# Three pairs of token tiles of the vs projection as seven block products, with weight sums built by adding transfers into SBUF

## The chip, the cores and the metric

The kernel runs on one core of one Trainium2 chip. The metric is the device time of that core in microseconds (us). Before the change the median of three runs is 911.1 us (910.71 to 911.81).

In what follows the engines carry the names of the profile: PE is the matrix engine, DVE the vector engine, ACT the scalar engine, POOL and SP the two engines that issue most of the DMA transfers.

## The reference, cut to what matters

```python
h = rmsnorm(x, norm_g[l])
proj = h @ w_in[l]
q, k, v, za, u, vs, zs, gm = jnp.split(proj, IN_SPLITS, axis=-1)
...
sgo = chunked_spatial_gating(jax.nn.gelu(u, approximate=False),
                             jax.nn.gelu(vs, approximate=False),
                             sg_w[l], sg_b[l], sg_ln_g[l], sg_ln_b[l])
```

`x` has 1024 tokens of 1024 features, in float32. The change concerns one part of `proj`: `vs`, 1024 columns, that is h (1024 x 1024) times a 1024 x 1024 block of `w_in`, followed by a gelu. The gating then layer-normalises vs over its features and mixes it over positions; u, the next projection, is computed right after vs.

## The kernel before

**Precision.** Each float32 operand is split into a high part and a low part. One ACT copy rounds the operand to the high part (`hi`), one DVE subtraction leaves the rest (`lo`); the helper `split` (lines 170 to 178) does both. A product then takes three matmuls: hi x hi, hi x lo and lo x hi. One matmul covers 128 tokens, a contraction of 128 and 512 output columns.

**Seven products.** Most projections of the kernel already use the scheme of Strassen and Winograd on 2 x 2 blocks (`gemm_pair`, line 405, `product`, line 382). The blocks of h are called b11, b21, b12, b22: feature half 0 or 1, token half 0 or 1. Five of the seven products need sums of those blocks or the last of them. The sums, t1 to t4, are made by `make_forms` (line 817) out of unrounded transposed copies of h (f11, f21, f12, f22); they serve the u projection, right after vs, and those that follow.

**vs, before.** vs is computed plainly, with 8 token tiles x 2 column halves x 8 contraction steps x 3 matmuls = 384 matmuls.

- *Column half 0* is computed while the eight tiles of x arrive. `normed_tile` (line 667) loads a tile of x, normalises and scales it (`scaled_part`, line 650, with the gain taken from the two PSUM banks `g_in`), transposes it on PE, casts it into hi and lo (`cast_part`, line 661) and copies the unrounded transpose to f11 to f22. `vs_gemm` (line 700) then runs the 24 matmuls of a tile into one PSUM bank, and line 706 copies it to `xh`. The weights of column half 0 lie split in SBUF in the slots T_t1 and T_t2 (`vs_split`).
- *Column half 1* follows in the loop at lines 857 to 869. There the eight tiles hold all eight PSUM banks at once; the outer loop runs over four weight tiles (`vs_weights`, line 795: one transfer of 512 KB, one cast, one subtraction), the inner one over the token tiles, with 6 matmuls for each. The work of `aside` (gelu of column half 0, `make_forms`) is emitted after every second tile.

**What orders the work.** The tile framework emits instructions by the order of the program unless they must wait, and puts later ones that are ready into gaps; each engine then executes its own queue strictly in order. Buffers of a tag are handed out in rotation: `wh` and `wl` (split weights) and `wr` (raw tiles of x and w) have three each, `s` two, `x` five; PSUM has four tags (mm, o, sc, tp) of two banks each. A transfer into a buffer waits for the last reader of its former content.

**Transfers.** Plain loads go through SP's queue (`copy_to`, line 227). Transfers that add to their destination go through POOL's queue (`add_to`, line 224). POOL's queue also carries the `early` steps (`early_job`, line 332, and line 516): sums of weight quarters for projections much later, made in DRAM. Each early step waits for the latest matmul of vs at the time it was emitted (`pace`), so that they are spread over PE's work; `part_of_early` (line 524) emits one of them at every second call.

**After vs** come the layer norm's statistics (`statistics_of`, line 901), `normalize` (line 905) and the mixing matmuls (`mix`, line 939), interleaved with `gemm_pair` of u, whose first weights are split in the last part of vs.

Of the kernel before, what the change touches and what calls it, by code (L numbers as in the profile page):

```python
# [32 lines left out]
P = 128  # L33
D = 1024
# [20 lines left out]
def hybrid_tile(  # L55
# [541 lines left out]
    for j in range(4):  # L597
# [25 lines left out]
    def quarter_of(t, j):  # L623

        if t >= 4 and j == 0:
            return b12[t - 4]
        return [v[:, :, tokens(t)] for v in hb[("b11", "b21", "b22")[j if t < 4 else 2]]]
# [22 lines left out]
    def scaled_part(t, j, xt, r):  # L650
        cs = half_of(j)
        scale = nc.vector.scalar_tensor_tensor(xt[:, cs], xt[:, cs], r[:], g_in[j][:], op0=ALU.mult, op1=ALU.mult)
        scalings.append(scale)
        pt = bank("o" if t == 1 else "tp")
        for i in range(4):
            k = j * 4 + i
            turn = nc.tensor.transpose(pt[:, i * P : (i + 1) * P], xt[:, k * P : (k + 1) * P], ident[:])
        p3 = pt[:].rearrange("p (k c) -> p k c", k=4)
        return p3, (f[f"f{j + 1}{t // 4 + 1}"][:, :, tokens(t)], p3), scale, turn
# [7 lines left out]
    def normed_tile(t, scale=None):  # L667
        xt, r = scale or scale_of(t)
        if t == 4:
            hb.update(new_b(("b22",)))  # L670
            f.update((n, slot(at, dt=F32)) for n, at in (("f12", "t4h"), ("f22", "t3h")))
        for j in range(2):
            p3, copy, _, _ = scaled_part(t, j, xt, r)
            cast_part(t, j, p3)
            nc.scalar.copy(*copy)

    def vs_step(acc, t, k, wh, wl):

        hi, lo = (v[:, k % 4, :] for v in quarter_of(t, k // 4))
        for n, (lt, rt) in enumerate(((hi, wh), (hi, wl), (lo, wh))):  # L680
            mm = nc.tensor.matmul(acc, lt, rt, start=k == 0 and n == 0, stop=k == KC - 1 and n == 2)  # L681
        return mm

    vs_w, vs_casts = [], []

    def split_vs(c):
# [11 lines left out]
        return cast, None  # L698

    def vs_gemm(t, middle=None):  # L700
# [19 lines left out]
    def first_tiles():  # L720
# [59 lines left out]
        high, low = cast_part(1, 1, p3)  # L780
        in_order(roots[2], high)
        vs_gemm(1, {4: lambda: both(3, "hl"), 5: lambda: normed_tile(2, third)})
        nc.scalar.copy(xh[:, 0, 0:HALF], acc0[:])
# [11 lines left out]
    def vs_weights(c):  # L795
        raw = raw_tile()
        nc.sync.dma_start(raw[:], w[W_VS + 4 + c])
        hi = mtile([P, D], F32R, "wh", 3)
        lo = mtile([P, D], F32R, "wl", 3)
        split(hi[:], lo[:], raw[:])  # L800
        return hi, lo

    def statistics(t, half):
        nc.vector.bn_stats(stats[:, t, half, :], xh[:, t, half_of(half)])

    def gelu_of(t):
        two = xh[:, t : t + 2, 0:HALF]
        after(nc.scalar.activation(two, two, AF.Gelu), roots[NT - 1])
        for i in range(2):
            statistics(t + i, 0)  # L810

# [5 lines left out]
    def make_forms():  # L817
# [17 lines left out]
        last = []  # L835
        for c in range(0, 4, 2):
            cs = slice(c, c + 2)
            v = mtile([P, 2, HALF], F32, "s", 2)
            nc.vector.tensor_sub(v[:], f11[:, cs, :], f21[:, cs, :])
            last.append(v)  # L840
            yield
        hb.update(new_b(("t3",)))
# [3 lines left out]
        hb.update(new_b(("t4",)))  # L846
        for c in range(0, 4, 2):
            form("t4", last[c // 2][:], c)
            yield

    accs = [bank(tag) for tag in ("mm", "mm", "o", "o", "sc", "sc", "tp", "tp")]
    aside = [lambda t=t: gelu_of(t) for t in range(0, NT, 2)]
    forms = make_forms()
    aside[1:1] = [lambda: next(forms, None)] * 2
    aside += [lambda: next(forms, None)] * 11
    weights = [vs_weights(0), vs_weights(1)]
    for c in range(4):
        if c + 2 < 4:
            weights.append(vs_weights(c + 2))
        for t in range(NT):  # L860
            wh, wl = weights[c]
            for k in range(2):
                ks = half_of(k)
                pace[0] = vs_step(accs[t][:], t, 2 * c + k, wh[:, ks], wl[:, ks])
            part_of_early()
            if c == 3:
                nc.scalar.activation(xh[:, t, HALF:D], accs[t][:], AF.Gelu)
            if aside and t % 2:
                aside.pop(0)()
    while aside:  # L870
# [1239 lines left out]
```

## Time and profile before

| | us |
|---|---|
| Median of three runs | 911.1 |
| The profiled execution, whole | 910.52 |
| Its span, first to last instruction | 908.7 |
| PE busy in the span | 898.6 |
| DVE busy | 693.3 |
| ACT busy | 528.6 |
| POOL busy | 145.6 |
| End of the vs projection on PE | 104.67 after the span's start |

All views of the profile come from one execution. Times are counted from the start of the span. A busy time is the time in which an instruction of that engine was executing; DMA-issuing instructions do not count. A view of "waits" names for each idle stretch of an engine what ended it; a "chain" is followed back from the last instruction through what released each step; a view of "windows" gives busy times for stretches of the span, with the number of instructions in brackets, the clock granted to PE, the mean busy share of the 16 DMA engines and the bytes that they moved.

### The profile page before, as it was taken

How to read it: one execution, taken by the hardware profiler on the slowest of the kernel's cores; microseconds unless marked ns; L12 is line 12 of the kernel's file. 1: busy time of each engine (PE TensorE's matmuls, PEld its weight loads, DVE VectorE, ACT ScalarE, POOL GpSimd, SP SyncE). 2: the span in 40 equal slices, each digit the busy share in tenths (PEclk: the TensorE clock that was granted, in tenths of full speed). 3: DMA queues.
4: the chain of work that ended last, by engine and by line, in shares of the span. 5: the costliest groups of instructions: out<-in, count | busy, mean ns of one | idle time of the engine just before them, and what ended most of it. 6: DMA issues, size and time to landing. Idle time of an engine off the chain costs nothing.

```text
span 908.7 us, 13248 instructions
## 1 busy us (share of the span) xinstructions
PE 898.6 (99%) x4305; PEld 748.9 (82%) x4305; DVE 693.3 (76%) x1238; ACT 528.6 (58%) x1060; POOL 145.6 (16%) x221
## 2 busy tenths in 40 slices
PE   8999999999999999999999999999999999999996
PEld 5788888888888888888888888888888888888885
DVE  6874776656678677888888887656698699579986
ACT  7942443334444557888778887434476485367443
POOL 2002222213011001222211110011100111210012
PEclk9999999999999999999999999999999999999999
DMA  6428788877778889999999994875568666998633
GB/s 232 139 93 216 170 163 190 178 186 222 241 263 267 268 265 319 266 256 270 270 344 252 269 241 144 300 261 182 171 208 301 221 203 179 283 323 282 201 116 116
DMA packets 129748, 206.10 MB, mean 227 GB/s; under 512 B 12716, under 2 KB 60848, under 8 KB 129680
## 3 DMA queue, kind: packets, MB, share of 16 engines
q1 hardware_dynamic: 108008, 146.27, 49.8%
q0 software_dynamic: 21376, 58.73, 26.7%
q8 instruction: 34, 0.56, 0.2%
q10 hardware_dynamic: 296, 0.27, 0.1%
q14 instruction: 34, 0.28, 0.1%
HBM read 148.46 MB, written 90.31 MB: 263 GB/s over the span
## 4 chain that ended last, share of the span: by engine, by line
PE 97%; DMA 1%; ACT 1%; DVE 0%; SPq 0%; issue 0%; ACTq 0%
PE ps_mm L395 44%; PE ps_o L395 27%; PE ps_mm L681 5%; PE ps_tp L395 4%; PE ps_sc L1291 3%; PE ps_sc L395 2%; PE ps_tp L943 2%; PE ps_tp L1372 2%; PE ps_o L1432 2%; PE ps_tp L681 1%; PE ps_sc L681 1%; PE ps_o L681 1%; PE ps_o L1440 1%; PE ps_tp L1382 1%; DMA T_t3h<-in_w_dram 1%; DMA wr<-in_x_dram 1%
## 5 line engine op out<-in xcount | busy, mean ns | idle before, releaser
L177 ACT CAST wh<-s 128x1024 fp32r<-128x1024 f32 (+1 forms) x78 | 78.1, 1003 | 82.6 <-PE ps_mm L395 29.0
L178 DVE TENSOR_TENSOR wl<-s,wh 128x1024 fp32r<-128x1024 f32 (+1 forms) x78 | 91.4, 1171 | 20.0 <-ACT wh L177 19.8
L178 DVE TENSOR_TENSOR wl<-wr,wh 128x1024 fp32r<-128x1024 f32 (+1 forms) x64 | 60.4, 945 | 59.1 <-ACT wh L177 58.9
L177 ACT CAST wh<-wr 128x1024 fp32r<-128x1024 f32 (+1 forms) x64 | 53.0, 830 | 77.5 <-PE ps_mm L395 34.5
L1332 ACT ACTIVATE pr<-ps_sc,sm 128x192 f32<-128x192 f32 (+2 forms) x128 | 51.3, 408 | 24.6 <-DVE sm L1323 21.6
L338 POOL DMA_DIRECT2D sums<-in_w_dram x48 | 36.7, 864 | 178.4 <-PE ps_mm L395 83.4
L395 PE MATMUL ps_o<-T_b22h,wh 128*128 128x512 f32 x148 | 59.0, 398 | 0.0
L395 PE MATMUL ps_o<-T_t1h,wh 128*128 128x512 f32 x148 | 58.0, 392 | 0.0
L395 PE MATMUL ps_o<-T_b22h,wl 128*128 128x512 f32 x148 | 57.8, 391 | 0.0
L395 PE MATMUL ps_o<-T_t1h,wl 128*128 128x512 f32 x148 | 57.8, 391 | 0.0
L395 PE MATMUL ps_o<-T_b22l,wh 128*128 128x512 f32 x148 | 57.8, 390 | 0.0
L395 PE MATMUL ps_o<-T_t1l,wh 128*128 128x512 f32 x148 | 57.7, 390 | 0.0
L395 PE MATMUL ps_mm<-T_t4h,wh 128*128 128x512 f32 (+1 forms) x144 | 55.9, 388 | 0.0
L395 PE MATMUL ps_mm<-T_t4l,wh 128*128 128x512 f32 (+1 forms) x144 | 55.4, 384 | 0.0
L395 PE MATMUL ps_mm<-T_t4h,wl 128*128 128x512 f32 (+1 forms) x144 | 55.3, 384 | 0.0
L395 PE MATMUL ps_mm<-T_t2h,wh 128*128 128x512 f32 x140 | 55.3, 395 | 0.0
L395 PE MATMUL ps_mm<-T_b11h,wh 128*128 128x512 f32 x140 | 55.1, 394 | 0.0
L395 PE MATMUL ps_mm<-T_t3h,wh 128*128 128x512 f32 x140 | 54.8, 391 | 0.0
L395 PE MATMUL ps_mm<-T_b11l,wh 128*128 128x512 f32 x140 | 54.7, 391 | 0.0
L395 PE MATMUL ps_mm<-T_b11h,wl 128*128 128x512 f32 x140 | 54.6, 390 | 0.0
L395 PE MATMUL ps_mm<-T_t3h,wl 128*128 128x512 f32 x140 | 54.6, 390 | 0.0
L395 PE MATMUL ps_mm<-T_t2h,wl 128*128 128x512 f32 x140 | 54.6, 390 | 0.0
(420 smaller groups left out, 2473.9 us busy)
## 6 DMA issues: line engine op xcount, KB each, us to landing
wr<-in_w_dram SPq DMA_DIRECT2D x80, 256.0 KB
sums<-in_w_dram POOLq DMA_DIRECT2D x24, 512.0 KB, 6.7
s<-sums SPq DMA_DIRECT2D x24, 512.0 KB
wr<-in_w_dram SPq DMA_DIRECT2D x16, 512.0 KB
q_hl<-qhl SPq DMA_DIRECT2D x16, 512.0 KB
q<-q_hl SPq DMA_DIRECT2D x64, 128.0 KB
y_dr<-x POOLq DMA_DIRECT2D x28, 256.0 KB, 6.4
sums<-in_w_dram POOLq DMA_DIRECT2D x24, 256.0 KB, 8.0
```

The source lines that it names most:

```text
L177: hi_casts.append(nc.scalar.copy(hi, src))
L178: return nc.vector.tensor_sub(lo, src, hi.bitcast(F32))
L338: return lambda: paced(nc.gpsimd.dma_start(dst, src, accum_op=op))
L395: mm = nc.tensor.matmul(acc, lt, rt, start=fresh and k == 0 and n == 0, stop=k == 3 and n == 2, skip_group_check=True,)
L681: mm = nc.tensor.matmul(acc, lt, rt, start=k == 0 and n == 0, stop=k == KC - 1 and n == 2)
L943: nc.tensor.matmul(pm[:, t * P : (t + 1) * P], xh[:, half * 4 + t, g * P : (g + 1) * P], bias[-1][1][:, g % 2, :], start=True, stop=True,)
L1291: nc.tensor.matmul(sc[:, i, lo:hi], q_of[:, c, i * P : (i + 1) * P], kt[:, f, lo:hi], start=f == 0, stop=f == 1,)
L1332: nc.scalar.activation(st.pr[:, i, place_of(c, lo, hi)], st.sc[c][:, i, lo:hi], AF.Exp, bias=st.nmax[:, c, i : i + 1], scale=-1.0, accum_o ...
L1372: nc.tensor.transpose(st.inner[0:wide, at : at + P], st.pr[:, i, place_of(c, 64 if st.t else P, 192)], ident[:])
L1382: nc.tensor.transpose(st.ends[0:wide, i * P : (i + 1) * P], st.pr[:, i, P : P + wide], ident[:])
L1432: nc.tensor.matmul(st.po[:], lt, rt, start=i == 0, stop=False, skip_group_check=True)
L1440: nc.tensor.matmul(st.po[:, cols(c)], ends[:, c, vs], st.b[:, cols(c)], start=False, stop=c == 1, skip_group_check=True)
```

## The change

- Token tiles p and p + 4 form a pair, for p = 1, 2, 3. The three pairs are computed with seven block products instead of eight. Tiles 0 and 4 stay plain.
- Column half 0 is now computed plainly for tiles 0 to 4 only. For tiles 1 to 3 the two contraction halves go to separate banks: the first half's product stays in its bank (`vs_acc`) for later use, a copy of it and the second half's product (bank `p1`, shared by the three) are added by DVE into `xh`.
- Column half 1 is computed plainly for tiles 0 and 4 only (`others`), with four weight tiles.
- Then come five products for each of the three pairs, in the order t1, t2, t3, b22, t4: the outer loop runs over the forms, then over two weight tiles for each, then over the three pairs, with 6 matmuls for each. `after_form` combines each finished product with `xh` on ACT or DVE and applies the gelu.
- The five products need five weights: W12+W22, W11+W12+W22, W11+W12, the sum of all four, and W22, in two tiles each. Three of them are built up in place in two SBUF tiles (`chain`, tag `s`): W12 is loaded, used by `others`, then W22, W11 and W21 are added one after another by adding transfers of 512 KB, each after the split of the former content. W11+W12 is built by a load and an adding transfer in a raw tile.
- The gain is copied from PSUM to SBUF (`g_sb`, two ACT copies) and taken from there from tile 2 on. The feature half 0 of tiles 5 to 7 is no longer cast to hi and lo. The t4 form is made in four x tiles instead of two s tiles. `make_forms` is emitted earlier.

```diff
-    b12 = [
-        [v[:].rearrange("p (a k c) -> p a k c", a=2, k=4)[:, i] for i in range(2)]
-        for v in (mtile([P, D], F32R, "s", 2) for _ in range(2))
-    ]
-    b12 = [(hi, mtile([P, 4, P], F32R, "x", 5)[:]) for two in b12 for hi in two]
+    b12 = [mtile([P, 4, P], F32R, "x", 5)[:] for _ in range(2)]
+    g_sb = htile([P, D], F32, "g_sb")
...
+            if t <= 4 or j:
+                cast_part(t, j, p3)
...
     def vs_gemm(t, middle=None):
-        acc = bank("mm")
+        acc = vs_acc[t] = bank("o" if t in (2, 3) else "mm")[:]
+        part = acc
+        if t == 1:
+            vs_acc["p1"] = bank("sc")[:]
+        dst = xh[:, t, 0:HALF]
         for k in range(KC):
             if middle and k in middle:
                 middle[k]()
-            vs_step(acc[:], t, k, *vs_w[k])
-        nc.scalar.copy(xh[:, t, 0:HALF], acc[:])
+            if t < 4 and k == 4:
+                nc.scalar.copy(dst, acc)
+                part = vs_acc["p1"]
+            vs_step(part, t, k, *vs_w[k], (0, KC - 1) if t == 4 else (k & 4, k | 3))
+        if t == 4:
+            nc.scalar.copy(dst, acc)
+        else:
+            nc.vector.tensor_add(dst, dst, part)
...
-    for t in range(NT):
+    chain = []
+    for t in range(5):
         if t > 1:
             vs_gemm(t)
         if t + 3 < NT:
             normed_tile(t + 3)
+        if t == 2:
+            for c in range(2):
+                chain.append(mtile([P, D], F32, "s", 2))
+                copy_to(chain[c][:], w[W_VS + 4 + c])
...
+    def of_chain(c, nxt=None):
+        two = vs_weights(chain[c][:])
+        if nxt is not None:
+            add_to(chain[c][:], w[W_VS + nxt])
+        return two
+
+    def of_raw(first, second=None):
+        raw = raw_tile()
+        copy_to(raw[:], w[W_VS + first])
+        if second is not None:
+            add_to(raw[:], w[W_VS + second])
+        return vs_weights(raw[:])
+
+    makers = [lambda c=c: of_chain(c, 6 + c) for c in range(2)]
+    makers += [lambda c=c: of_raw(6 + c) for c in range(2)]
+    makers += [lambda c=c: of_chain(c, c) for c in range(2)]
+    makers += [lambda c=c: of_chain(c, 2 + c) for c in range(2)]
+    makers += [lambda c=c: of_raw(c, 4 + c) for c in range(2)]
+    makers += [lambda c=c: of_chain(c) for c in range(2)]
+    makers += [lambda c=c: of_raw(6 + c) for c in range(2)]
...
+    for _ in range(2):
+        more_weights()
+    others = {t: bank("sc")[:] for t in (0, 4)}
     for c in range(4):
-        if c + 2 < 4:
-            weights.append(vs_weights(c + 2))
-        for t in range(NT):
-            wh, wl = weights[c]
+        more_weights()
+        wh, wl = weights[c]
+        for t in (0, 4):
             for k in range(2):
-                ks = half_of(k)
-                pace[0] = vs_step(accs[t][:], t, 2 * c + k, wh[:, ks], wl[:, ks])
-            part_of_early()
+                pace[0] = vs_step(others[t], t, 2 * c + k, wh[:, half_of(k)], wl[:, half_of(k)])
             if c == 3:
-                nc.scalar.activation(xh[:, t, HALF:D], accs[t][:], AF.Gelu)
-            if aside and t % 2:
-                aside.pop(0)()
+                nc.scalar.activation(xh[:, t, HALF:D], others[t], AF.Gelu)
+            part_done()
+
+    t5s = {1: bank("tp")[:], 2: bank("tp")[:], 3: vs_acc[4]}
+
+    def after_form(name, p, acc):
+        q1, q2 = xh[:, p + 4, 0:HALF], xh[:, p + 4, HALF:D]
+        if name == "t1":
+            nc.scalar.mul(q2, acc, -1.0)
+        elif name == "t2":
+            nc.scalar.copy(q1, acc)
+        elif name == "t3":
+            nc.vector.tensor_sub(q2, q2, acc)
+            gelu_of(p + 4, 1, 1)
+        elif name == "b22":
+            nc.vector.tensor_add(q1, q1, acc)
+            gelu_of(p + 4, 1)
+        else:
+            nc.scalar.activation(xh[:, p, HALF:D], acc, AF.Gelu, scale=-1.0)
+
+    for s, name in enumerate(("t1", "t2", "t3", "b22", "t4")):
+        into = t5s if name in ("t1", "b22") else vs_acc
+        for c in range(2):
+            more_weights()
+            wh, wl = weights[4 + 2 * s + c]
+            hi, lo = hb[name]
+            for p in (1, 2, 3):
+                for k in range(2):
+                    at = 2 * c + k
+                    pace[0] = step_of(
...
+                if c:
+                    after_form(name, p, into[p])
+                part_done()
```

`part_done` calls `part_of_early` and emits the next piece of `aside`; `more_weights` makes the next entry of `makers`, so that weights are requested two weight tiles ahead of their use. `step_of` holds the three matmuls of a step.

More of the change, by code (lines that the diff above doesn't have):

```diff
@@ L673, in normed_tile, with step_of, vs_step @@
             p3, copy, _, _ = scaled_part(t, j, xt, r)
-            cast_part(t, j, p3)
+            if t <= 4 or j:
+                cast_part(t, j, p3)
             nc.scalar.copy(*copy)
-    def vs_step(acc, t, k, wh, wl):
+    def step_of(acc, hi, lo, wh, wl, first, last):
+        for n, (lt, rt) in enumerate(((hi, wh), (hi, wl), (lo, wh))):
+            mm = nc.tensor.matmul(
+                acc, lt, rt, start=first and n == 0, stop=last and n == 2, skip_group_check=True
+            )
+        return mm
+    def vs_step(acc, t, k, wh, wl, ends=(0, KC - 1)):
         hi, lo = (v[:, k % 4, :] for v in quarter_of(t, k // 4))
-        for n, (lt, rt) in enumerate(((hi, wh), (hi, wl), (lo, wh))):
-            mm = nc.tensor.matmul(acc, lt, rt, start=k == 0 and n == 0, stop=k == KC - 1 and n == 2)
-        return mm
+        return step_of(acc, hi, lo, wh, wl, k == ends[0], k == ends[1])
     vs_w, vs_casts = [], []
@@ L781, in first_tiles @@
         in_order(roots[2], high)
+        for j in range(2):
+            nc.scalar.copy(g_sb[:, half_of(j)], g_in[j][:])
         vs_gemm(1, {4: lambda: both(3, "hl"), 5: lambda: normed_tile(2, third)})
@@ L846, in make_forms @@
         hb.update(new_b(("t4",)))
[L847 to L852, printed above, removed]
-    forms = make_forms()
-    aside[1:1] = [lambda: next(forms, None)] * 2
-    aside += [lambda: next(forms, None)] * 11
-    weights = [vs_weights(0), vs_weights(1)]
+        hi, lo = hb["t4"]
+        for c in range(4):
+            split(hi[:, c, :], lo[:, c, :], last[c][:])
+            if c % 2:
+                yield
```

60 lines of the change are left out of this document (43 added, 17 removed).

## The prediction

> **What bounds the kernel now.** I read the page first, then the waits of PE, then the chain that ended last, and then the busy times in windows around the vs projection.
>
> ```profile
> span 908.7 us, 13248 instructions
> PE 898.6 (99%) x4305; PEld 748.9 (82%) x4305; DVE 693.3 (76%) x1238; ACT 528.6 (58%) x1060; POOL 145.6 (16%) x221
> PE 97%; DMA 1%; ACT 1%; DVE 0%; SPq 0%; issue 0%; ACTq 0%
> ...
> PE ps_o L591 <- DVE T_b22l L106: 1.5, 1, 1.5
> PE ps_mm L754 <- ACT T_t2h L692: 0.7, 1, 0.7
> PE ps_sc L599 <- DVE wh L585: 0.6, 1, 0.6
> PE ps_tp L657 <- ACT T_t3h L675: 0.2, 1, 0.2
> PE ps_mm L754 <- ACT T_b11h L663: 0.2, 1, 0.2
> ```
>
> PE is busy 99% of the span and makes 97% of the chain. The second part of the fence is the view of waits for PE alone: in the whole execution PE waits five times, 3.2 us in all, each time on lines of the first tiles. So a matmul that is left out saves its own duration, as long as nothing else is late. The chain and the windows show the place:
>
> ```profile
> 44.81 19.06 PE ps_mm L681 x84
> ...
> 101.95 2.72 PE ps_tp L681 x12
> 104.67 2.72 PE ps_mm L395 x12
> ...
> 121.24 1.78 PE ps_tp L943 x16
> ```
>
> ```profile
> 0.00:44.80 44.80, 41.53 (x202) 30.68 (x203) 34.59 (x77) 38.66 (x72) 6.49 (x19) 1.00 0.54 185
> 44.80:104.67 59.87, 59.87 (x266) 49.57 (x265) 37.55 (x47) 22.44 (x29) 9.61 (x15) 1.00 0.61 172
> 63.87:104.67 40.80, 40.80 (x181) 33.78 (x181) 23.86 (x32) 12.59 (x16) 9.61 (x15) 1.00 0.77 209
> ```
>
> The columns of the windows are the length, then busy time and instructions of PE, weight loads, DVE, ACT and POOL, the granted clock (1.00), the share of the DMA engines and GB/s. From 44.80, when tile 4 of column half 0 and the last transposes are done, to 104.67 PE runs 264 matmuls of vs (tiles 5 to 7 with 24 each, then 192) without a gap: 59.87 / 264 = 0.2268 us each, at full clock. DVE is used for 37.55 us of this stretch (63%), ACT for 22.44, the DMA engines for 61%, and for 77% in its later part. These three must take up whatever the change adds.
>
> **The change part by part.**
>
> *Matmuls removed.* Per pair, 8 block products of 12 matmuls become 7. The code leaves 5 x 24 + 48 + 5 x 36 = 348 matmuls of 384; three block products, 36 matmuls, are gone: 36 x 0.2268 = 8.16 us. That is certain, since every matmul has the same shape as before. Up to 44.80 the count is as before (tiles 0 to 4), so this is PE's calendar without waits: column half 1 of tiles 0 and 4 from 44.80, a weight tile every 12 matmuls (2.72 us); t1 from 55.69, each form 36 matmuls (8.16 us), a weight tile every 4.08; t2 from 63.85, t3 from 72.02, b22 from 80.18, t4 from 88.34, end 96.51 instead of 104.67.
>
> *Up to 44.80.* Added: three DVE additions, two ACT copies of the gain; removed: three casts and three subtractions of the same half-tile size. DVE has 10 us free there and ACT 6 (first row of the windows), and PE's only wait after the first 13 us is the 0.2 us one. I cost this at nothing; the cover is that tile 4 was cast long before its matmuls. Without it each costs its own half-tile duration, some 0.6 us.
>
> *Weight splits.* From 44.80 on, before, two vs weight tiles are split; now twelve. What one takes, and how closely DVE operations follow each other:
>
> ```profile
> 72.06 1.05 ACT L177 CAST wh<-wr 128x1024 fp32r<-128x1024 f32 x1 [2.55 <-PE ps_tp L681]
> 73.15 1.23 DVE L178 TENSOR_TENSOR wl<-wr,wh 128x1024 fp32r<-128x1024 f32 x1 [4.26 <-ACT wh L177]
> ...
> 50.08 2.35 DVE L822 TENSOR_TENSOR T_t3l<-T_t3l,T_t4h 128x1024 f32<-128x1024 f32 x2
> ...
> 89.79 0.69 DVE L282 TENSOR_TENSOR s<-wr 128x512 f32<-128x512 f32 x1
> 90.39 0.69 DVE L279 TENSOR_TENSOR s<-wr,wr 128x512 f32<-128x512 f32 x1
> ```
>
> From the cast's start to the end of the subtraction is 2.32 us. In a run of them DVE needs 2.35 - 1.23 = 1.12 us for a full tile and 0.60 for a half one.
>
> *DVE's balance.* Added after 44.80: ten subtractions (11.2 us) and six combinations of `after_form` (3.6); one subtraction of tile 7 is gone (-0.6). 37.55 + 14.2 = 51.8 us, in a stretch of 51.71: on paper full. But not all of it is due in this stretch: it also holds six pieces of `statistics_of` (0.68 + 0.21 us each) and two half-tile sums for the second u pair (0.60 each), some 6.5 us, and these are due only before the mixing:
>
> ```profile
> L804 DVE BATCH_NORM_STATS2 bn<-xh 128x6 f32<-128x512 f32 x15 | 9.8, 676 | 1.8 <-ACT xh L867 1.1 <-ACT xh L808 0.7
> ...
> L903 DVE BATCH_NORM_AGGREGATE mv<-bn 128x2 f32<-128x12 f32 x6 | 1.2, 207 | 0.1
> ...
> 114.68 1.53 DVE L908 TENSOR_SCALAR xh<-xh,mv,st 128x1024 f32<-128x1024 f32 x2
> ```
>
> The normalisation ends at 116.2 and the mixing starts at 121.24 (in the chain above), 5.0 us to spare. What must be done before 96.51 is 45.3 us, 88%. Then from 96.51 DVE would start up to 6.5 us in arrears against 5.0 us to spare: a loss between 0 and 1.5 us. I take 0, since 6.4 us of the stretch are free for some of these pieces, and one quarter of them used is enough. ACT gets ten casts and seven to eight more half-tile operations, 22.4 + 10.5 + 5 = 38 of 51.7 us: no bound.
>
> *t1's form.* It is due at 55.69, not 12 matmuls after 104.67. In the trace its first step, a subtraction, starts at 50.08 (row above); cast and subtraction follow, so its first half stands at 50.08 + 1.2 + 2.3 = 53.6, and could be earlier, since the slots that it waited for come free after tile 4 instead of tile 7. The two more splits ahead of it on DVE cost 2.2 us, less the 0.6 saved on tile 7: 55.2. Just in time, so nothing; if it is pushed by another split, 1 us.
>
> *The adding transfers.* Eight of 512 KB each, plus four more loads of that size. No transfer that adds into SBUF is in this trace. The nearest rows are transfers of the same size that add into DRAM (the two views are the DMA issues from 480 to 545 us, and the instructions of line 518), and the early steps:
>
> ```profile
> g<-in_w_dram POOLq DMA_DIRECT2D x4, 512.0 KB, 8.2
> ...
> DMA to landing us min/median/max: 5.8/7.3/8.9
> ...
> q0 software_dynamic: 157, 0.58, 48.9%
> ```
>
> ```profile
> sums<-in_w_dram POOLq DMA_DIRECT2D x14, 512.0 KB, 5.5
> ...
> DMA to landing us min/median/max: 4.5/6.7/16.7
> ```
>
> An adding transfer of 512 KB lands 8.2 us after its issue, where the DMA engines are nearly full and one is in flight at a time; POOL's queue then takes 48.9% of a window of 8 us (490 to 498), so about 3.3 us of all engines for one, after some 0.6 for the store that shares it. The early copies land after 5.5, and the slowest early step shown after 16.7.
>
> Which of them PE must wait for: W22 into the chain is harmless. Nothing holds back the load of W12, and loads without a condition go out early, as this one that belongs to code far behind vs does:
>
> ```profile
> 8.89 0.43 SPq L878 DMA_DIRECT2D bm_sb<-in_b_merge_dram  x1
> ```
>
> The link that is tight is W11. The buffer for t1's first weight comes free when the second weight of column half 1 is done, at 50.24; its split ends at 52.56; only then may W11 be added; the sum must then be split again by 63.85. That leaves 63.85 - 2.32 - 52.56 = 8.97 us for the transfer. W21, the next link, has 14.0 us by the same reckoning, counted with the delay that W11 leaves behind. With a landing time L the loss is (L - 9.0) + (L - 14.0), each at least 0.
>
> How long is L there? In front of it in POOL's queue are the early steps, now from about 47 us on, one every 2.72 us, and the two transfers that build W11+W12, whose raw buffers come free at about 45 and 48. So I add one adding transfer that lies ahead: 8.2 + 3.3 = 11.5 us, a loss of 2.5. The ends: 5.8 (no loss) and 16.7 (7.7 + 2.7 = 10.4). POOL itself loses nothing, since only issues are queued behind W11; an early step behind it goes out a little later, and these sums are needed far later.
>
> The Trainium skill, "DMA: Bandwidth & Descriptors", section "Anatomy of one DMA", gives 2.0 us plus bytes / 436 GB/s for a transfer of POOL's queue; by it L would be 3.2 us and the loss 0. The trace disagrees already for plain copies (5.5 us), so I don't go by it. The Trainium skill, on the same page, section "SWDGE vs HWDGE vs iDMA", says that POOL's transfers have only one queue, which speaks for adding what lies ahead; no row here shows the order inside the queue.
>
> *Sum.* On the profiled execution's own time: 910.52 - 8.16 + 2.5 = 904.9; it lies 0.6 below the median of the runs, so **905.4 us** against 911.1.
>
> **The rivals.**
>
> *A, the forecast:* W11 late by 1 to 4.6 us, everything else covered: 903.9 to 907.5.
>
> *B, all is hidden:* L stays under 9.0, as the median of 8.2 says, and DVE keeps up: 911.1 - 8.2 = 902.9. For it: PE never waits after the start today. Against it: eight adding transfers in 50 us, where that median was measured with one at a time.
>
> *C, DVE becomes the bound:* it is 88 to 100% booked and works strictly in order, so a wait for a cast can no longer be made up. The longest such wait in this stretch is 4.26 us (the row at 73.15). One of them passed on to PE on top of A gives 905.4 + 4.3 = 909.7. Against it: in the trace these waits arise because DVE has nothing else to do.
>
> *D, slower:* the adding transfers are as slow as the slowest row. Their demand speaks for it: 8 x 3.3 = 26 us of all DMA engines, on top of 0.61 x 59.87 = 36.5 that the stretch needs already, is more than 51.7. Then the two links cost 10.4 us: 911.1 - 8.16 + 10.4 = 913.3. It decides from L = 15.6 on, where the two losses reach 8.16. Against it: part of the demand lies before 44.80, where the DMA engines are 54% busy, and the early steps wait for PE when PE waits.
>
> That the change doesn't do what it says can be left out: the count of matmuls is fixed by the code.
>
> **How the numbers follow.** A 0.45, B 0.24, C 0.16, D 0.15. The time is that of A. Differences within 0.2% (1.8 us, 909.3 to 912.9) can't be told from no change here. Faster: A, B and half of C, 0.77; same: the other half of C, 0.08; slower: D, 0.15. The range goes from B, less the 0.4 us by which the fastest run lies under the median, 902.5, to C with A's own spread and the 1 us of t1's form added (909.7 + 2.1 + 1), 912.8; it leaves out D and little else. A alone is 903.9 to 907.5.
>
> **What would show it right or wrong.** PE with 36 matmuls fewer, u's first matmul at about 99 (96.5 if B holds). One wait of PE of 1 to 5 us where t2 begins, on the split of a weight out of `s`, which itself waits for a transfer on POOL's queue: then the W11 link is as computed. Waits on DVE at form starts with the transfer long landed mean C, as does a mixing that waits for the normalisation; waits at both t2 and b22 with landing times over 15 us mean D; no wait at all is B. The prediction would be wrong in its reasoning if PE waited before 44.80, or if PE lost time only after u has begun.

## The result, and the profile after

The changed kernel takes 915.44 us (median of 14 runs, 913.27 to 920.34), the kernel before 911.43 in the runs beside it. The ratio is 1.0048, with a 95% interval of 1.0034 to 1.0062: about 4 us slower, where the prediction had 6 us faster and a range that ends at 912.8. The second measurement gave 915.17 us and 1.0051 [1.0032, 1.0070].

The execution profiled first (span 918.5) was the longest of its 14 runs: 3.7 us of it are one wait at 249.86 us that the second profile doesn't have. So the stages are read from the second one (span 913.8 against 908.7, 5.1 us more). First its page, then its view of the waits of PE (us in total, times, longest):

```profile
span 913.8 us, 13256 instructions
PE 895.6 (98%) x4269; PEld 744.8 (82%) x4269; DVE 705.1 (77%) x1258; ACT 539.3 (59%) x1076; POOL 152.3 (17%) x229
PE 85%; DVE 6%; DMA 5%; ACT 2%; issue 1%; SPq 0%; DVEq 0%; ACTq 0%
```

```profile
PE ps_mm L678 <- ACT wh L177: 2.6, 1, 2.6
PE ps_mm L395 <- ACT x L427: 1.8, 1, 1.8
PE ps_tp L1045 <- DVE xh L1010: 1.5, 2, 0.8
PE ps_o L591 <- DVE T_b22l L106: 1.5, 1, 1.5
PE ps_tp L1045 <- DVE x L1061: 1.4, 1, 1.4
PE ps_tp L655 <- ACT T_t3h L674: 0.9, 1, 0.9
```

PE runs 4269 matmuls, the 36 fewer that the change promises, and yet the span is longer. The larger new waits are in two places: L678 is the matmul of the forms of vs, and L395, L1045 with L1010 and L1061 belong to the first pair of u, with its normalisation and mixing. The chain that ended last shows both, with what was late (columns: start, length, what):

```profile
54.40 12.05 DMA s<-in_w_dram
66.53 1.05 ACT wh L177
67.60 1.24 DVE wl L178
68.89 2.50 PE ps_mm L678 x5
...
91.92 6.91 DMA wr<-in_w_dram
...
105.38 7.11 DMA wr<-in_w_dram
```

*The first place, t2.* The first adding transfer of W11 is issued at 54.40 and takes 12.05 us to land; cast and subtraction follow, and PE starts t2 late. The windows around it (columns as in the prediction):

```profile
64.83:67.62 2.79, 0.15 (x1) 0.00 (x0) 0.02 (x1) 1.04 (x1) 0.00 (x0) 1.00 1.07 305
67.62:69.50 1.88, 1.31 (x3) 0.71 (x4) 1.88 (x2) 0.00 (x0) 0.37 (x1) 0.54 1.01 296
69.50:74.17 4.67, 4.67 (x12) 3.61 (x11) 3.05 (x5) 3.66 (x6) 2.37 (x4) 0.50 1.01 231
74.17:76.20 2.03, 2.03 (x9) 1.65 (x8) 1.71 (x3) 2.03 (x3) 1.08 (x2) 0.90 1.06 317
```

PE stands for 2.79 us, and then it runs at about half of the full clock (0.54, 0.50) until shortly after 74.17. Matmuls of t2 lie 0.43 us apart in that stretch instead of 0.227. t3's first matmul is at 79.60 where the calendar, counted from t1's start at 56.66, has 72.99: t2 costs 6.6 us. t2's first two matmuls start at 67.62 and 68.89. Counted from start to start they come 2.79 and 1.04 us late, 3.8 us together (the timeline gives 2.64 and 0.57, since it counts idle time from the end of the matmul before). The 35 matmuls from 68.89 on take 2.8 us more than at 0.227 each; that is the slower clock. From 79.60 to u's first matmul at 104.08 are 24.48 us, three forms of 8.16: no more is lost in vs. Before t1 another 0.97 us is lost (56.66 against 55.69); most of it is the wait of 0.9 us on the copy T_t3h at L674, where the kernel before waits 0.2.

*The second place, the first pair of u.* The two rows are the windows of the 84 matmuls from u's first one on, of the kernel before and of the changed one, counted at line 395 alone:

```profile
104.67:127.33 22.66, 19.51 (x84) 15.30 (x84) 1.00 0.88 134
```

```profile
104.08:132.65 28.57, 19.95 (x85) 15.40 (x84) 1.00 0.77 149
```

The same work takes 5.9 us longer, at full clock. DVE's timeline says why (start, length, operation, and in brackets the idle time before it with what ended it). First the second pair's sum in the kernel before, then the changed kernel:

```profile
97.36 0.69 DVE L282 TENSOR_TENSOR s<-wr 128x512 f32<-128x512 f32 x1 [0.63 <-DMA wr<-in_w_dram]
```

```profile
98.92 0.69 DVE L282 TENSOR_TENSOR s<-wr 128x512 f32<-128x512 f32 x1 [3.33 <-DMA wr<-in_w_dram]
...
112.58 0.69 DVE L282 TENSOR_TENSOR s<-wr 128x512 f32<-128x512 f32 x1 [4.14 <-DMA wr<-in_w_dram]
...
115.00 0.16 DVE L161 TENSOR_SCALAR st<-mv 128x8 f32<-128x8 f32 x1
```

L282 makes the sums of weight quarters for a pair of u out of raw tiles (`wr`). DVE stands there for the transfers of u's first and second pair, and behind the second in its strict order are the normalisation (L161, then L1010), which the mixing on PE needs. In the kernel before, the first pair's sums were begun at 89.79, 15 us before u (row in the prediction), and the second pair's sum waited 0.63 us; here the first pair's come 5 us before u, and the second's wait 4.14. t4's raw W22 tiles now hold the raw buffers that u's loads need: they are read by the splits at 90.31 and 93.17, the first pair's load goes out at 91.92, right after the first of these, and the second pair's load (105.38) waits in turn for the first pair's sums.

The account on the profiles: -8.16 (matmuls) + 0.97 + 6.6 (t2) + 5.9 (first pair of u) = +5.3; the span grew by 5.1.

### The profile page after: what moved, and what is told of

The parts are those of the page before. It is cut to its first block, busy times and chain, and to the rows that moved or that the text cites. A ratio compares the mean times of both kernels' runs of the same rounds, so it can differ in the third digit from the quotient of the medians.

```text
span 918.5 us, 13256 instructions
## 1 busy us (share of the span) xinstructions
PE 895.6 (98%) x4269; PEld 744.5 (81%) x4269; DVE 704.4 (77%) x1258; ACT 537.8 (59%) x1076; POOL 152.7 (17%) x229
## 3 DMA queue, kind: packets, MB, share of 16 engines
HBM read 154.76 MB, written 90.31 MB: 267 GB/s over the span
## 4 chain that ended last, share of the span: by engine, by line
PE 84%; DMA 6%; DVE 5%; ACT 2%; issue 2%; SPq 1%; POOL 0%; ACTq 0%; DVEq 0%; POOLq 0%
PE ps_mm L395 41%; PE ps_o L395 24%; PE ps_tp L395 4%; PE ps_sc L1393 3%; PE ps_sc L395 2%; DMA wr<-in_w_dram 2%; DVE wl L178 2%; PE ps_tp L1474 2%; PE ps_o L1534 2%; PE ps_tp L1045 1%; DMA s<-in_w_dram 1%; PE ps_o L1542 1%; PE ps_tp L1484 1%; DMA T_t3h<-in_w_dram 1%; PE ps_sc L678 1%
## 5 line engine op out<-in xcount | busy, mean ns | idle before, releaser
L177 ACT CAST wh<-s 128x1024 fp32r<-128x1024 f32 (+1 forms) x86 | 86.4, 1007 | 85.2 <-PE ps_mm L395 25.2
L178 DVE TENSOR_TENSOR wl<-s,wh 128x1024 fp32r<-128x1024 f32 (+1 forms) x86 | 100.6, 1170 | 25.0 <-ACT wh L177 24.8
L178 DVE TENSOR_TENSOR wl<-wr,wh 128x1024 fp32r<-128x1024 f32 (+1 forms) x66 | 62.9, 954 | 57.0 <-ACT wh L177 57.0
L177 ACT CAST wh<-wr 128x1024 fp32r<-128x1024 f32 (+1 forms) x66 | 55.0, 835 | 65.3 <-PE ps_mm L395 37.7
L395 PE MATMUL ps_mm<-T_t2h,wh 128*128 128x512 f32 x140 | 56.0, 400 | 3.7 <-ACT x L417 3.7
L395 PE MATMUL ps_o<-T_b22h,wh 128*128 128x512 f32 x148 | 59.0, 398 | 0.0
L395 PE MATMUL ps_o<-T_t1h,wh 128*128 128x512 f32 x148 | 58.1, 392 | 0.0
L395 PE MATMUL ps_o<-T_b22h,wl 128*128 128x512 f32 x148 | 57.8, 391 | 0.0
L395 PE MATMUL ps_o<-T_t1h,wl 128*128 128x512 f32 x148 | 57.8, 391 | 0.0
L395 PE MATMUL ps_o<-T_b22l,wh 128*128 128x512 f32 x148 | 57.8, 390 | 0.0
L395 PE MATMUL ps_o<-T_t1l,wh 128*128 128x512 f32 x148 | 57.7, 390 | 0.0
L395 PE MATMUL ps_mm<-T_t3h,wh 128*128 128x512 f32 x140 | 54.9, 392 | 1.6 <-ACT x L427 1.6
L395 PE MATMUL ps_mm<-T_t4h,wh 128*128 128x512 f32 (+1 forms) x144 | 55.8, 387 | 0.0
L395 PE MATMUL ps_mm<-T_t4h,wl 128*128 128x512 f32 (+1 forms) x144 | 55.3, 384 | 0.0
L395 PE MATMUL ps_mm<-T_t4l,wh 128*128 128x512 f32 (+1 forms) x144 | 55.3, 384 | 0.0
L395 PE MATMUL ps_mm<-T_t2l,wh 128*128 128x512 f32 x140 | 55.2, 394 | 0.0
L395 PE MATMUL ps_mm<-T_b11h,wh 128*128 128x512 f32 x140 | 55.1, 394 | 0.0
L395 PE MATMUL ps_mm<-T_t2h,wl 128*128 128x512 f32 x140 | 55.1, 394 | 0.0
L395 PE MATMUL ps_mm<-T_b11l,wh 128*128 128x512 f32 x140 | 54.7, 391 | 0.0
L395 PE MATMUL ps_mm<-T_b11h,wl 128*128 128x512 f32 x140 | 54.6, 390 | 0.0
```

Source lines behind the costliest of these rows:

```text
L177: hi_casts.append(nc.scalar.copy(hi, src))
L178: return nc.vector.tensor_sub(lo, src, hi.bitcast(F32))
L395: mm = nc.tensor.matmul(acc, lt, rt, start=fresh and k == 0 and n == 0, stop=k == 3 and n == 2, skip_group_check=True,)
```

## The experiments

Ratios are to the kernel before, measured beside each, with the 95% interval.

**The changed kernel once more.**

> The changed kernel once more, for a second profile beside the timing. Theory: 4 us above the kernel before (ratio about 1.0045), with PE waiting where t2 begins (the transfer that adds W11 lands more than 9 us after its issue) and again in the first u pair, because the first sum of the second u pair stands in DVE's order ahead of the normalisation and waits for a load. The wait of 3.7 us at 249 us in the first profile, in the queries' stage, is chance by this theory and is gone in this profile. Rival: that late wait is a third loss of the change, and is there again.

915.17 us, 1.0051 [1.0032, 1.0070]. It is the profile read above.

**The W11 adds left out.** The two weights that contain W11 by way of the chain are then not the sums.

```diff
-    makers += [lambda c=c: of_chain(c, c) for c in range(2)]
+    makers += [lambda c=c: of_chain(c) for c in range(2)]
```

> Leaves out the two transfers that add W11, so that the weights of t2 and of the sum of all four lack W11; all else is as in the changed kernel. Theory: no wait of PE at t2, the loss there (3.8 us of waiting, 1.8 us at half clock behind it) goes, 5 to 6.5 us less than the changed kernel, about 909.5. Rival DVE: DVE is what t2 waits for, PE waits there as long as before and the time stays at 915. Rival of the full DMA engines: the wait moves on to b22, and at most 2 us are gained.

909.69 us, 0.9991 [0.9978, 1.0004]: 5.5 us less than the changed kernel, most of the 6.6 lost at t2. t2 waits for nothing, and u begins at 99.99. But DVE now stands 6.63 us at the first L282, which costs PE 3.1 us at u's start, and the 84 matmuls take 26.9 us. So the second place isn't a consequence of the first.

**The second pair's sums behind the normalisation.** The first sum of u's second pair is ordered behind the last L1010 on DVE; nothing else is moved.

```diff
-            nc.vector.tensor_scalar(
+            norm_end[0] = nc.vector.tensor_scalar(
...
+        if first is None and norm_end[0] is not None:
+            first, norm_end[0] = norm_end[0], None
```

> The sums of the second u pair are ordered behind the normalisation on DVE; nothing else changes. Theory: DVE no longer stands still for 4 us just before the statistics' square root, the waits of PE between 109 and 131 us shrink from 8 us to under 3, 4 to 5.5 us less than the changed kernel, about 910.5. Rival: DVE has simply too much work there, the order does not matter, and the time stays within 1 us of 915.

912.32 us, 1.0019 [1.0005, 1.0034]: 2.9 us less, not quite the 4 expected. The 84 matmuls take 24.2 us instead of 28.6, with the same instructions on DVE. It was the order that cost, not their number. (u itself begins at 103.11 here, 1 us earlier.) Part of the gain is lost again later: this profile has PE waits of 0.45 us at 211.87 and 0.71 at 242.83, where the changed kernel's has none.

**A clear queue for W11.** No early step until t3 and then one with every part; the adds of W11+W12 behind those of W11 in POOL's queue.

> No early step is emitted before t3 (made up for afterwards, one for every part), and the two transfers that build W11+W12 are ordered behind those that add W11. Theory: the adding transfer is slow because of what lies ahead of it in POOL's queue; W11 lands within 9 us, PE does not wait at t2, 5 to 6.5 us less than the changed kernel, about 909.5. Rival: a transfer that adds into SBUF takes over 12 us by itself, PE waits at t2 as before, and the time stays at 915.

920.40 us, 1.0107 [1.0088, 1.0127]: a miss. W11 lands in 5.4 us and t2 waits for nothing, as intended. But the postponed steps then come out every 1.36 us from 74.85 on, and u's loads meet them. DVE's timeline:

```profile
99.74 0.69 DVE L282 TENSOR_TENSOR s<-wr 128x512 f32<-128x512 f32 x1 [10.74 <-DMA wr<-in_w_dram]
116.83 0.69 DVE L282 TENSOR_TENSOR s<-wr 128x512 f32<-128x512 f32 x1 [7.59 <-DMA wr<-in_w_dram]
```

What t2 gained is given back with interest in u.

**Three ways of mending single places, early steps as they were.** First the order of the adds alone:

```diff
-            add_to(raw[:], w[W_VS + second])
+            after(add_to(raw[:], w[W_VS + second]), link[1])
```

> The adding transfers into the raw W11+W12 tiles (51.15 and 52.45 us in the trace of after) are issued on POOL behind the two W11 adds instead of ahead of them; nothing else is moved. Theory (the W11 link is late because other adding transfers stand ahead of it in POOL's queue): with two transfers of 512 KB fewer ahead, the W11 add lands in 8 to 10 us instead of 12.5, the tensor engine's wait at the first matmul of t2 shrinks from 2.6-3.1 us to under 1, u begins 2 to 4 us earlier; time 911 to 913. What is lost in u's first pair stays. Rival (all transfers share the engines, the order is nothing): the landing stays at 12 us and the time at 915.

919.49 us, 1.0089 [1.0067, 1.0111]: 4 us worse than the change itself. In the profile the W11 add now lands in 8.4 us and t2 waits 0.7 us. t3 has a wait of 6.0 us in its place. From the chain:

```profile
54.47 8.38 DMA s<-in_w_dram
...
70.53 14.30 DMA wr<-in_w_dram
84.83 0.02 issue
84.86 1.05 ACT wh L177
```

The second add of W11+W12 came to stand behind the W21 adds and three early steps in POOL's queue, went out at 70.53 and took 14.30 us, with these just ahead of it. t3 needed it.

Then a raw buffer of its own for t4's first W22 tile (`spare`), so that u's first pair can load earlier; alone, and with the sums' order:

```diff
-    makers += [lambda c=c: of_raw(6 + c) for c in range(2)]
+    makers += [lambda c=c: of_raw(6 + c, raw=(spare, None)[c]) for c in range(2)]
```

> The raw tile of t4's first W22 weight gets a buffer of its own, so that the raw buffer which the first pair of u loads into is free before t4's splits. Theory (the vector engine's in-order wait at the sums of u's first and second pair, L282, comes from raw buffers freed late): the first pair's wait of 3.3 us at L282 goes, the second pair's of 4.0 us shrinks by 1 to 3, and of the 5.6 us lost in u's first 84 products 2 to 4 come back; time 911 to 913.5; the wait at the start of t2 stays. Rival (these loads are late because the queues are full, not for a buffer): L282 still waits 3 us for each pair; time 915.

> The buffer of its own together with the sums of u's second pair ordered behind the normalisation on the vector engine. Theory: both late sums leave the normalisation alone, the first 84 products of u take 23 us as in the kernel before instead of 28.4; what is left of the loss is that of t2; time 909.5 to 911.5. Rival (the second ordering alone gave all there is to gain): 912.3, as with the ordering alone.

923.88 us (1.0122 [1.0105, 1.0140]) and 914.34 us (1.0032 [1.0020, 1.0044]): both miss. With the buffer alone the tile framework put the first pair's sums earlier in DVE's order than their load landed:

```profile
92.50 0.69 DVE L282 TENSOR_TENSOR s<-wr 128x512 f32<-128x512 f32 x1 [6.44 <-DMA wr<-in_w_dram]
...
116.63 0.69 DVE L282 TENSOR_TENSOR s<-wr 128x512 f32<-128x512 f32 x1 [7.65 <-DMA wr<-in_w_dram]
```

DVE stood 6.44 us before 92.50, ahead of a weight split of b22 that PE then waited 1.9 us for, and 7.65 us for the second pair, where PE waited 6.7. Together with the sums' order the first 84 matmuls of u take 24.2 us, as that order alone gives; b22's wait of 1.7 us stays. The buffer did let the first pair's sums begin earlier (92.50 against 98.92), as the account of the raw buffers has it. But an earlier free buffer is no gain while the order on DVE counts on a faster load.

All three at once:

> Three orders at once: W11 adds ahead of the raw W11+W12 adds on POOL, the buffer of its own for t4's first raw W22 tile, and the second pair's sums behind the normalisation. Theory (the loss has two separate places, t2 and u's first pair): the gains add up, t2 loses under 2 us and u's first 84 products take 23 us; time 905 to 909, below the kernel before. Rival (a transfer moved up makes another late, so the gains don't add): 910 to 912.

915.82 us, 1.0047 [1.0035, 1.0060]: the gains don't add up; t3 waits 5.6 us, by the same late add of W11+W12 (issued at 71.44).

**Adding or bytes.** Which part of the 12 us is the adding itself?

```diff
-        nc.gpsimd.dma_start(dst, src, accum_op=ALU.add)
+        nc.gpsimd.dma_start(dst, src)
```

> The eight adding transfers become plain loads of the same 512 KB from the same queue at the same places: what they fetch replaces what stood there, so the sums of weight quarters are left out. Theory (what counts is that 512 KB more must pass a full set of DMA engines): W11 still lands 11 to 13 us after its issue, the waits at t2 and in u's first pair stay, time 913 to 916. Rival (adding into SBUF is itself dear): W11 lands in 6 to 9 us, the wait at t2 is under 1 us, time 908 to 911.

> All eight adding transfers are left out, so the weights of the forms are not the sums; every split, every matmul and every load stays. Theory (the transfers are the whole loss): no wait at t2, u begins at 97 to 99 us, u's first 84 products take 23 to 25 us, time 903 to 907. Rival (the ten more weight splits and the combinations fill the vector engine, as the prediction's C has it): u's first pair still loses 3 to 5 us, time 907 to 911.

909.53 us (0.9996 [0.9975, 1.0016]) with plain loads in place of the adding transfers, 909.06 us (0.9979 [0.9968, 0.9991]) without any; in both, the weights of the forms are not the sums. My theory that only the bytes count falls: by the medians, plain loads of the same bytes at the same places bring back 5.6 of the 6.1 us that leaving them out brings. The cost of one transfer is best read where W22 is added, alone in POOL's queue. The view of the DMA queues from 25 to 35 us, changed kernel first, then plain loads (q0 is POOL's queue; packets, MB, share of 16 engines; then the issues with their median to landing):

```profile
q0 software_dynamic: 265, 1.00, 55.3%
...
s<-in_w_dram POOLq DMA_DIRECT2D x2, 512.0 KB, 6.9
```

```profile
q0 software_dynamic: 288, 1.05, 28.9%
...
s<-in_w_dram POOLq DMA_DIRECT2D x2, 512.0 KB, 4.5
```

An adding transfer of 512 KB takes 5.53 us of all engines for each MB (55.3% of 10 us / 1.00 MB), a plain one 2.75: twice as much, and 2.4 us more to land.

For W11 itself the traces give more than the difference of the two. These are the landing times of its two transfers (shortest, median, longest, in us): the changed kernel, plain loads at the same places, and, from the last group of runs below (906.95 us), adding transfers with only each other ahead in POOL's queue:

```profile
DMA to landing us min/median/max: 12.0/12.6/13.2
DMA to landing us min/median/max: 8.6/8.7/8.9
DMA to landing us min/median/max: 5.4/5.4/5.4
```

Adding as such doesn't make W11 late: 5.4 us is well inside the 8.97 us of the prediction. What is late is an adding transfer behind others. With the early steps ahead but not W11+W12 (the order of the adds alone) the two land in 8.4 and 8.7 us, with W11+W12 ahead but no early step (early steps from part 15 on, below) in 8.6 and 9.1, with both in 12.0 and 13.2.

Neither kernel comes near 903. Without any add PE runs vs to the calendar (u's first matmul at 96.85), but the 84 matmuls of u take 27.4 us, since DVE still stands for the second pair's load ahead of the normalisation:

```profile
104.15 0.69 DVE L282 TENSOR_TENSOR s<-wr 128x512 f32<-128x512 f32 x1 [4.76 <-DMA wr<-in_w_dram]
```

**Fewer early steps in vs, and the sums behind the normalisation.** The changed kernel emits an early step with every second of 38 parts (19 steps; the kernel before had 16 in vs, from 64 us on). Here they begin with part 7 or with part 15; in the second case the rest is made up in the attention stage.

```diff
     def part_done():
-        part_of_early()
+        parts[0] += 1
+        if parts[0] > 6:
+            part_of_early()
```

> The early steps of the vs stage are put off until t1 is done (from its end on every second part as before, about 12 instead of 19 in vs; the rest is made up much later, in the attention stage), and the sums of u's second pair stand behind the normalisation. Theory (early steps of 512 KB and adding transfers together overfill the DMA engines between 45 and 75 us): W11 lands in 6 to 9 us, the wait at t2 is under 1 us, u begins at 97 to 100 us and its first 84 products take at most 25 us; time 905 to 909. Rival (the early steps only come out later and delay the loads of u instead, as when they were piled up behind t2): 912 or more.

> As the kernel before it in this group, but the early steps of the vs stage begin with the seventh part (16 in vs, as many as in the kernel before the change) and nothing is made up later. Theory: a step less ahead of the W11 adds; the wait at t2 is 1 to 2 us, time 909.5 to 911.5, between the ordering of the sums alone (912.3) and the kernel that puts off more. Rival (the place of the early steps is nothing): 912.3.

From part 15 on: 912.55 us (1.0018 [1.0003, 1.0034]); from part 7 on: 910.24 us (0.9988 [0.9976, 0.9999]). In the first, u begins at 100.91, but t2 still waits 0.7 us for W11, which has the W11+W12 adds ahead in its queue and lands in 9.1. Its profiled execution, the longest of the ten (915.87), also has a wait of 2.5 us for a reload of q in attention (L1401), where the postponed steps are made up.

**Both causes away.** Plain loads in place of adding ones (so that the weights are not the sums), the sums behind the normalisation, early steps from part 7 on.

> Both suspected causes taken away at once: the eight adding transfers are plain loads of the same size (the sums of weight quarters are left out), the sums of u's second pair stand behind the normalisation, the early steps begin with the seventh part of vs. Theory (two separate causes: an adding transfer takes more of the DMA engines than a plain one, and the vector engine's in-order wait for u's loads ahead of the normalisation): no wait over 0.7 us at t2, u begins at 97 to 98 us and its first 84 products take 23 to 24.5 us; time 904 to 907, near the calendar of 903. Rival (in u's first pair the vector engine simply has too much work, as the prediction's C has it): u's first pair still loses over 3 us, 908 to 910.

904.27 us, 0.9922 [0.9909, 0.9935]: inside the expectation, though the rival allowed 908 at least. u begins at 96.85 and its 84 matmuls take:

```profile
96.85:120.60 23.75, 19.67 (x84) 15.46 (x84) 1.00 0.91 152
```

DVE is busy for 704.5 us in it, as in the kernel without adds (704.8), which takes 4.8 us longer. So too much work on DVE isn't the second loss. That its order is rests on the run with the sums behind the normalisation, which changed nothing else; here the early steps were put off too.

**A version whose weights are the sums.** The order of the adds, the early steps from part 15 on at the old pace, and the sums behind the normalisation; beside it, early steps from part 11 on without that order.

> The adding transfers for W11+W12 behind those of W11, the early steps of vs put off until t1 is done, and u's second sums behind the normalisation. Theory: with nothing ahead of it in POOL's queue W11 lands in 6 to 8 us and t2 waits for nothing; W11+W12 lands before t3 needs it, since no early step is beside it; time 906.5 to 909.5. Rival (the adding transfers of t3 and b22 and u's loads meet the early steps later on): 911 to 914.

> Early steps of vs from the eleventh part on, u's second sums behind the normalisation, a few steps made up in the attention stage. Theory: between the starts with part 7 (910.2) and part 15 (912.6 with an accidental wait in attention): 909 to 911. Rival (making up steps in attention costs by itself): 912 to 913.

> The kernel with the early steps from the seventh part on and u's second sums behind the normalisation once more, in five rounds, to see whether it stands below the kernel before the change: 909 to 911.5 by its first measurement (910.24 against 911.05). Rival: 912.3, as with the order of the sums alone.

906.95 us for the first, 0.9963 [0.9950, 0.9977]: it beats the changed kernel by 8 us and the kernel before by 4. Its POOL timeline and the waits of PE:

```profile
55.03 0.86 POOL L225 DMA_DIRECT2D s<-in_w_dram  x1 [7.79 <-DVE wl L178]
57.90 0.86 POOL L225 DMA_DIRECT2D s<-in_w_dram  x1 [2.00 <-DVE wl L178]
58.50 2.03 POOL L225 DMA_DIRECT2D wr<-in_w_dram  x2
63.12 0.86 POOL L225 DMA_DIRECT2D s<-in_w_dram  x1 [2.59 <-DVE wl L178]
...
68.64 0.76 POOL L342 DMA_DIRECT2D sums<-in_w_dram  x1
```

```profile
PE ps_o L595 <- DVE T_b22l L106: 1.5, 1, 1.5
PE ps_tp L1055 <- DVE x L1071: 1.2, 1, 1.2
PE ps_tp L659 <- ACT T_t3h L678: 0.9, 1, 0.9
```

W11 goes first, W11+W12 directly behind it, and no early step until 68.64: no wait at t2 or t3 is left (L682 doesn't appear), and u begins at 98.14, 1.6 us after the calendar. What is left against 903 lies mostly in u's first pair: 25.93 us for the 84 matmuls, with DVE still standing 4.72 us at the first L282. The order of the adds alone cost 4 us, and the putting-off with the sums' order gave 912.55; together they give 906.95. How much of these last 5.6 us is the order of the adds isn't shown, since the profile of 912.55 also has the wait in attention, and this one has none there.

From part 11 on: 920.72 us, 1.0101 [1.0087, 1.0116], a miss of 10 us. Its profile shows 7.1 us of DVE at the first L282 and 4.4 us of PE in attention, where the steps are made up (its waits, then its window there):

```profile
PE ps_sc L1401 <- DMA q<-q_hl: 4.4, 2, 3.7
```

```profile
500.00:562.00 62.00, 57.58 (x304) 49.16 (x303) 46.06 (x113) 44.91 (x130) 6.98 (x9) 0.94 0.81 223
```

The kernel of 906.95 us makes up more steps in attention and waits for none there (62.00 us of PE in that window). Why some placements collide with the reload of q and others don't, these runs leave open. The repeated measurement of the part-7 kernel gave 909.99 us, 0.9986 [0.9976, 0.9997]: a real but small gain on the kernel before.

## Why the prediction was wrong, point by point

- *Matmuls removed, -8.16 us:* right. 36 fewer, and with no adding transfer at all PE keeps the calendar to 0.3 us (u at 96.85 against 96.51).
- *Up to 44.80 at nothing:* nearly. PE waits 0.9 us for the copy T_t3h of tile 7 at 45.49. ACT has no more to do up to 44.80 than before (38.27 against 38.66 us), but now a gelu (L856, from 43.89) stands right ahead of this copy in its order. The prediction gave ACT 6 us to spare but didn't ask when.
- *t1's form just in time:* right; no wait at t1 in any profile read here.
- *The W11 link:* right as to the place, the wait and its cause, and the landing was 12.05 us against an estimated 11.5. The price was mis-sized. The estimate took 2.5 us, W11 late and nothing else; measured are 6.6. Of these some 3.8 are lateness: the 2.5, 0.55 for the landing, and 0.9 because W11 was issued at 54.40 instead of 52.56 + 0.97, after a split that came behind one of t1's form on DVE. The other 2.8 us are the halved clock behind the wait, for which the sum has no term. The prediction's rows had no such wait in a dense stretch, so no row showed that a wait of 2.8 us can cost more than itself. That POOL's transfers have only one queue, which the prediction cites from the Trainium skill ("DMA: Bandwidth & Descriptors", section "SWDGE vs HWDGE vs iDMA"), is in keeping with W11's landings of 5.4 us with nothing ahead and 12.05 behind other transfers. The formula that the Trainium skill gives on the same page, section "Anatomy of one DMA", 3.2 us, lies under every landing of these transfers: the fastest of the plain loads into `s` took 3.8, the fastest add 5.3.
- *The price of adding:* right in size. It was taken as 3.3 us of all engines per transfer from adds into DRAM; W22's cost 2.9 (5.53 us for a MB, 0.52 MB each), twice a plain load. But the conclusion, one add ahead and the early steps harmless, was too mild. The prediction gave the demand of 62.5 us in a stretch of 51.7 to its rival D. Measured from 44.80 to 104.08 is a DMA share of 0.95, 56 us against 36.5 before, and moving single transfers moved the lateness on to another user: from W11 to W11+W12 (the order of the adds alone), or to u's loads (the clear queue).
- *DVE's balance at 0 to 1.5 us:* here the prediction failed. It asked how much work DVE has and compared it with the normalisation's 5 us of room. It did not ask on which transfers DVE waits in order. The missing step is that weight tiles of vs, t4's two W22 tiles last, hold the raw buffers up to the end of vs, so that u's first sums, which had been begun 15 us ahead of u, begin 5 us ahead, and that the second pair's sums stand ahead of the normalisation on DVE. That cost 5.9 us, where the sum has nothing, and moving that order with the amount of work unchanged brought 4.4 of it back.
- *"The prediction would be wrong in its reasoning if ... PE lost time only after u has begun":* somewhat under half of the loss (5.9 of 13.5 us) is of that kind, and about half (6.6) is at t2, where the forecast had a wait.
- *Rivals:* C named DVE and its strict order, but as an engine full of work that passes on waits for casts; what it passed on were waits for loads. The sign that it gave did appear: the mixing waited 1.5 us for the normalisation. D had the right sign and about the right size (913.3 against 915.4), but by W11 landing after 16.7 us and W21 late behind it; W11 took 12.05, and PE never waited for W21. That its figure lies near is luck. Neither is what happened.

## What to carry to other kernels

When PE's work ahead of a stage shrinks, look at every load of the next stage: which buffer it waits for, who now reads that buffer last, and what stands behind its first user on an in-order engine. Count adding transfers at twice their bytes, put the one that is needed first ahead of the others and of fillers in the queue, and move the fillers to a stretch that has room, at the old pace. A wait inside a dense run of matmuls can cost more than its length (6.6 us for 3.8 here), and a reordering that only moves a late transfer shows as the same loss one stage on.

## What the hardware showed that was not expected

- Behind t2's waits of 2.64 and 0.57 us PE's granted clock was halved for about 6.6 us (0.50 from 69.50 to 74.17), and matmuls of 512 columns then started 0.427 us apart. The Trainium skill, "TensorE: Matmul & The Clock Gate", section "Part 1: The HAM clock gate (the "warmup" mystery)", gives 426.7 ns for that state, and the trace agrees; it gives an idle window of about 3.4 us as what brings the state on, and here a shorter gap did. The length of a wait alone doesn't settle it: with the spare buffer, a wait of 1.89 us at 94.39 was followed by a clock of 0.50 (95.3 to 98.6), while the changed kernel's wait of 1.81 us at 116.94 left it at 1.00. What decides isn't shown.
- An adding transfer into SBUF occupies the DMA engines twice as long as a plain one of the same bytes (5.53 against 2.75 us for a MB) and lands in 6.9 instead of 4.5 us alone in POOL's queue, with SP's loads beside it (28.6 and 43.4% of the engines' time). Behind other adding transfers and early steps it landed in 12 to 14 us.
